# The down projection in two pairs of column blocks, with mixed pairs of contraction tiles, and three mixed pairs in ten gate/up units

## The chip, the core and the metric

One core of a Trainium2 chip runs the whole program, a two-layer decoder trunk in one launch. The metric is the device time of one execution in microseconds (us); the median of three runs is given. A profile is one execution recorded by the hardware profiler. Its engines are PE (TensorE: the matrix engine), DVE (VectorE), ACT (ScalarE), POOL (GpSimd) and SP, which issues most of the DMAs.

## What is computed

The input has 256 tokens of 2048 numbers, all float32. Each layer adds a normed mixer and a normed feed-forward part (FFN). Layer 0 has an SSD (Mamba-2) mixer, layer 1 has attention in a sliding window. Only the FFN is touched here:

```python
def swiglu(u, w_gate, w_up, w_down):
    return (jax.nn.silu(u @ w_gate) * (u @ w_up)) @ w_down
...
    ffn = swiglu(rmsnorm(h, g[2]), ffn_w_gate[layer], ffn_w_up[layer], ffn_w_down[layer])
    h = h + rmsnorm(ffn, g[3])
```

`w_gate` and `w_up` are 2048 x 5632, `w_down` is 5632 x 2048.

## The kernel before

**Products.** Tokens lie in two blocks of 128 (t = 0, 1). A weight tile of 128 contraction rows and 512 columns multiplies a block of tokens as three matmuls, since every float32 is held as a high and a low part in a shorter form: x_hi with w_hi, x_hi with w_lo, x_lo with w_hi. One such triple is called a product below.

**Weights.** `Weights` streams them. `specs` lists the loads in the order of use. `_load` fetches the next raw tile (512 KB: two contraction tiles of 512 columns) into one of RAWB = 5 buffers, up to four ahead; SP issues the DMAs in order. `_convert` makes `whi` with a cast on ACT and `wlo` with a subtraction on DVE, each in CVB = 4 buffers, three ahead of PE. A buffer is free for the next load or conversion when its last reader is done. A plain raw tile is one conversion of 128x1024, and 12 matmuls.

**The mixed form.** For two token blocks, two column blocks (in gate/up: 512 columns of gate and the same 512 of up) and a pair of contraction tiles (e, o), plain products would be eight. `mixed_unit` computes seven from sums of weights and differences of tokens (Strassen's scheme). Two raw tiles, `a` and `b`, carry the four weight tiles, each fetched by two DMAs of 256 KB. `_mixed` then gives four things to convert: `a` itself, t13 (one DVE add of 128x1024 from a and b), t24 (two DVE adds of 128x512, from t13, a and b), and `g`, half of b. They feed two, two, two and one products. The differences of tokens come once per layer from `mixed_x`, into `sx`. The seven banks p1 to p7 and `up1` are joined at the end of the unit by DVE (`L700` to `L703` once the mixed pairs are over, and `L708`), then SiLU on ACT and the product on DVE (`L712`).

**The FFN of a layer.** Gate and up go through 11 units of 512 columns. Unit 0 runs plain while h, the residual stream, is being updated (`a_first`); units 1 to 8 (S_FIRST to S_LAST) are mixed, with SPAIRS = 2 mixed pairs out of eight pairs of contraction tiles; units 9 and 10 are plain. The output of a unit is transposed on PE (`store_half`) and split into hh and hl; the part of units 8 and on goes to a second pair of tiles (`late`), which take the room of the mixed form's buffers. `mix_stage` then does down plain: four blocks of 512 columns, each with 44 contraction tiles and two token blocks. Behind each block, ACT takes the sum of squares (`squares`) and DVE multiplies with the norm's weights (`post`); the last block runs its last tiles token block by token block, so that the first one's norm factor is ready early. `add_residual` then updates h. `hook` starts small jobs (`mixed_x`, `store`) between weight tiles.

**Order.** A scheduler orders each engine's instructions at build time from the program order and priorities; at run time an engine runs its list in order, and semaphores hold it where data or a buffer is not ready. So an instruction that waits holds up everything behind it on its engine.

Of the kernel before, what the change touches and what calls it, by code (L numbers as in the profile page):

```python
# [30 lines left out]
SPAIRS = 2  # L31
S_FIRST, S_LAST = 1, 8
LATE = 8


class Weights:
# [40 lines left out]
    def _mixed(self, i, part):  # L77
# [57 lines left out]
def tile_yoco(ctx: ExitStack, tc: tile.TileContext, a: dict):  # L135
# [39 lines left out]

    def add_ffn(l):
        wg, wu = a["ffn_w_gate"][l], a["ffn_w_up"][l]
        for u in range(FF // CW):
            if not S_FIRST <= u <= S_LAST:
# [3 lines left out]
            for i in S_ORDER:  # L183
                e = SUB * i
                if i < SPAIRS:
                    for part, first, second in (("a", (wg, e), (wu, e + 1)), ("b", (wg, e + 1), (wu, e))):
                        specs.append(("s%d_%d" % (l, u), (part, *(wap(w, k, 1, CW * u, CW) for w, k in (first, second)))))
                else:
                    specs.append(("gate%d_%d" % (l, u), wap(wg, e, SUB, CW * u, CW)))
                    specs.append(("up%d_%d" % (l, u), wap(wu, e, SUB, CW * u, CW)))  # L190
        for c in range(4):
            add("down%d_%d" % (l, c), a["ffn_w_down"][l], KF, CW * c)
# [279 lines left out]
    h = hpool.tile([P, NT, D], F32, tag="h", name="h")  # L472
    for t in range(NT):
        nc.sync.dma_start(h[:, t, :], x[P * t : P * (t + 1), :])

    def mix_stage(key, xt, kts, layer, which, bk0=None, hook=None, lag=2):


        xh, xl = xt[:2]
        gpost = load_g(hpool, norm_w[layer, which], "gpost")  # L480
        ss = [hpool.tile([P, 4], F32, tag="mss%d" % t, name="mss", bufs=2) for t in range(NT)]
        bks = []

        def squares(bk, c, t):
            junk = hpool.tile([P, CW], mybir.dt.bfloat16, tag="junk", name="junk", bufs=2)
# [761 lines left out]
```

## Time and profile before

| | us |
|---|---|
| median of three runs | 2410.99 (2410.32 to 2412.8) |
| the profiled execution | 2411.38 |
| its span in the trace | 2409.7 |
| layer 0, SSD stage | 0 to about 690 |
| layer 0, gate and up | about 691 to 1187 |
| layer 0, down | about 1187 to 1416 |
| attention | 1417 to 1675 |
| layer 1, FFN | 1676 to 2401 |
| last norm, update of h, output | 2401 to 2409.7 |

The profile's page gives busy times, a picture of the span in slices, the DMA queues, the chain of waits and the costliest groups of instructions. The chain of waits starts at the last instruction and goes back, at each step, to what released it; the engine that holds most of it sets the time. A matmul's row in the trace is longer than the distance to the next one, because matmuls overlap in the engine's pipeline; the distance of the starts is the pace. Line numbers such as L672 are those of the code above. Buffer numbers are left out in the trace, so t13 and t24 both read `t`.

### The profile page before, as it was taken

To read this page: it belongs to the slowest core of one execution; us is meant where nothing else is said; L and a number is where in the kernel's file an instruction comes from. 1 tells how busy PE (TensorE), PEld (TensorE's weight loads), DVE (VectorE), ACT (ScalarE), POOL (GpSimd) and SP (SyncE) were. 2 spreads that over 40 slices of the span, in tenths; PEclk is the share of its full clock that TensorE was granted. 3 is DMA by queue.
4 is the path that set the end of the run, shared out by engine and by line. 5 is a ranking of instruction groups with operands and counts; after the bars stand their busy time and mean duration, and the time that the engine had idled before them with its cause. 6 is when DMAs were issued, how large, how long until landed. Compare 5 with 4: busy or idle time off the path is not lost.

```text
span 2409.7 us, 31424 instructions
## 1 busy us (share of the span) xinstructions
PE 2390.0 (99%) x11714; PEld 1980.7 (82%) x11714; DVE 1667.9 (69%) x2329; ACT 1279.7 (53%) x1805; POOL 87.2 (4%) x66
## 2 busy tenths in 40 slices
PE   9999999999999999999999999999999999999998
PEld 8888888888878888888888878777888888888887
DVE  6998878875577878875444468865878778554444
ACT  6566766654464545544444457755545555444443
POOL 2500100000000000000000000000000000000000
PEclk9999999999999999999999999999999999999999
DMA  7666666657656565666666664445665656666664
GB/s 223 184 202 192 186 190 191 183 178 244 193 165 200 177 216 168 216 201 185 207 193 194 194 191 153 128 126 163 191 202 177 214 177 199 201 189 207 194 194 143
DMA packets 285434, 453.80 MB, mean 188 GB/s; under 512 B 18000, under 2 KB 116560, under 8 KB 284512
## 3 DMA queue, kind: packets, MB, share of 16 engines
q1 hardware_dynamic: 284960, 451.39, 60.9%
q8 instruction: 92, 1.51, 0.3%
q14 instruction: 62, 0.51, 0.1%
q10 hardware_dynamic: 288, 0.33, 0.0%
q0 software_dynamic: 32, 0.07, 0.0%
HBM read 449.56 MB, written 2.16 MB: 187 GB/s over the span
## 4 chain that ended last, share of the span: by engine, by line
PE 97%; ACT 1%; DVE 1%; issue 0%; POOL 0%; DVEq 0%; POOLq 0%; ACTq 0%
PE bank L291 14%; PE bank L350 14%; PE bank L351 14%; PE bank L349 14%; PE bank L672 9%; PE bank L673 9%; PE bank L671 9%; PE bank L296 7%; PE bank L644 1%; PE bank L949 1%; PE bank L1125 1%; PE bank L1168 1%; DVE wlo L115 1%; PE bank L411 1%; ACT xx L270 0%; PE bank L1160 0%
## 5 line engine op out<-in xcount | busy, mean ns | idle before, releaser
L115 DVE TENSOR_TENSOR wlo<-raw,whi 128x1024 fp32r<-128x1024 f32 (+1 forms) x785 | 936.1, 1200 | 568.8 <-ACT whi L114 567.6
L114 ACT CAST whi<-raw 128x1024 fp32r<-128x1024 f32 (+1 forms) x785 | 811.1, 1036 | 828.9 <-PE bank L351 506.3
L291 PE MATMUL bank<-xx,whi 128*128 128x512 f32 (+1 forms) x1488 | 523.3, 396 | 0.0
L296 PE MATMUL bank<-xx,wlo 128*128 128x256 f32 (+1 forms) x1488 | 416.1, 285 | 0.0
L672 PE MATMUL bank<-wlo,xx 128*128 128x512 f32 x864 | 336.9, 390 | 0.3 <-DVE wlo L115 0.2
L671 PE MATMUL bank<-whi,xx 128*128 128x512 f32 x864 | 337.2, 393 | 0.0
L673 PE MATMUL bank<-whi,xx 128*128 128x512 f32 x864 | 336.9, 390 | 0.0
L291 PEld LDWEIGHTS bank<-xx,whi 128*128 128x128 f32 (+1 forms) x1488 | 276.6, 188 | 61.2 <-issue 0.4
L296 PEld LDWEIGHTS bank<-xx,wlo 128*128 128x128 f32 (+1 forms) x1488 | 280.2, 188 | 11.4 <-issue 7.0
L349 PE MATMUL bank<-whi,hh 128*128 128x512 f32 x512 | 199.3, 389 | 0.0
L351 PE MATMUL bank<-whi,hl 128*128 128x512 f32 x512 | 199.2, 389 | 0.0
L350 PE MATMUL bank<-wlo,hh 128*128 128x512 f32 x512 | 199.2, 389 | 0.0
L672 PEld LDWEIGHTS bank<-wlo,xx 128*128 128x128 f32 x864 | 162.3, 188 | 35.2 <-DVE wlo L115 2.1
L673 PEld LDWEIGHTS bank<-whi,xx 128*128 128x128 f32 x864 | 162.2, 188 | 34.2
L671 PEld LDWEIGHTS bank<-whi,xx 128*128 128x128 f32 x864 | 162.2, 188 | 32.8
L349 PE MATMUL bank<-whi,xx 128*128 128x512 f32 x416 | 162.6, 393 | 2.5 <-ACT xx L270 2.1
L351 PE MATMUL bank<-whi,xx 128*128 128x512 f32 x416 | 162.5, 392 | 0.9 <-DVE xx L271 0.9
L350 PE MATMUL bank<-wlo,xx 128*128 128x512 f32 x416 | 162.3, 391 | 0.5 <-DVE wlo L115 0.5
L114 ACT CAST whi<-t 128x1024 fp32r<-128x1024 f32 x64 | 67.2, 1050 | 107.7 <-DVE t L91 49.8
L351 PEld LDWEIGHTS bank<-whi,hl 128*128 128x128 f32 x512 | 96.1, 188 | 20.1
L350 PEld LDWEIGHTS bank<-wlo,hh 128*128 128x128 f32 x512 | 96.1, 188 | 20.0
L349 PEld LDWEIGHTS bank<-whi,hh 128*128 128x128 f32 x512 | 96.1, 188 | 19.7
(222 smaller groups left out, 3157.4 us busy)
## 6 DMA issues: line engine op xcount, KB each, us to landing
raw<-in_ffn_w_down_dram SPq DMA_DIRECT2D x176, 512.0 KB, 4.9
raw<-in_ssm_w_in_dram SPq DMA_DIRECT2D x161, 512.0 KB, 4.6
raw<-in_ffn_w_gate_dram SPq DMA_DIRECT2D x144, 512.0 KB, 4.5
raw<-in_ffn_w_up_dram SPq DMA_DIRECT2D x144, 512.0 KB, 4.6
raw<-in_ssm_w_out_dram SPq DMA_DIRECT2D x64, 512.0 KB, 4.8
raw<-in_ffn_w_gate_dram SPq DMA_DIRECT2D x64, 256.0 KB, 3.2
raw<-in_ffn_w_up_dram SPq DMA_DIRECT2D x64, 256.0 KB, 3.7
raw<-in_attn_w_q_dram SPq DMA_DIRECT2D x32, 512.0 KB, 3.4
```

Source lines behind the costliest of these rows:

```text
L114: self.pin(nc.scalar.copy(hi[:], src))
L115: self.pin(nc.vector.tensor_tensor(lo[:], src, hi[:].bitcast(F32), ALU.subtract))
L291: nc.tensor.matmul(o, wh, xx[:, kt, :, :].rearrange("p a t -> p (a t)"), start=(kt == 0), stop=(kt == kts - 1))
L296: nc.tensor.matmul(o[:, :T], wl, xx[:, kt, 0, :], start=False, stop=False)
L349: nc.tensor.matmul(o, sh, wh, start=(kt == 0), stop=False)
L350: nc.tensor.matmul(o, sh, wl, start=False, stop=False)
L351: nc.tensor.matmul(o, sl, wh, start=False, stop=(kt == kts - 1))
L411: nc.tensor.matmul(o[:], hi[:, kk, cs], xr[2][:, kt, :, :].rearrange("p a t -> p (a t)"), start=(kt == 0), stop=(kt == KD - 1))
L644: nc.tensor.transpose(pt[:, P * k : P * (k + 1)], scr[:, NT + t, P * k : P * (k + 1)], ident[:])
L671: nc.tensor.matmul(o, sh, wh, start=(n == 1), stop=False)
L672: nc.tensor.matmul(o, sh, wl, start=False, stop=False)
L673: nc.tensor.matmul(o, sl, wh, start=False, stop=(n == total[name]))
```

## The change

Three things change in the FFN of each layer.

Gate and up: units 1 to 10 are now mixed, with three mixed pairs (SPAIRS = 3) of eight. The order within a unit is a list: `UNIT` = A3 B3 M0 A4 B4 M1 A5 B5 M2 E A6 B6 A7 B7, where A and B are a plain raw tile of gate and of up, M a mixed pair, and E the first joining of the banks.

Down: the four column blocks go as two pairs, in the same form. `DOWN[0]` has six mixed pairs and 32 plain raw tiles: eight lead, then each M is followed by three. `DOWN[1]` has eight mixed pairs and 28 plain tiles: two lead, then each M is followed by two. Differences of tokens (now of hh and hl) are made by `mixed_x` for six and two pairs. The first half is kept in SBUF (`res`) after its norm weights, and copied back into banks near the end.

Room: hh and hl are now whole from the start, so h does not fit beside them. `spill_h` writes it to DRAM (`hd`) after `a_first` of unit 0 by two DMAs of 1 MB from POOL; `fetch_h` brings it back near the end of down, from POOL too. And t24 has no tile of its own any more: the two adds write into the raw tile `a`.

```diff
-SPAIRS = 2
-S_FIRST, S_LAST = 1, 8
-LATE = 8
+SPAIRS = 3
+def both(*pairs):
+    return [(c, i) for i in pairs for c in "AB"]
+def down_order(npairs, lead, each, last_a):
+    rest = range(npairs, KF // SUB)
+    a_ = [("A", i) for i in rest]
+    b_ = [("B", i) for i in rest]
+    n = lead + each * npairs
+    na = len(a_) - last_a
+    subs = a_[:na] + b_[: n - na]
+    seq = subs[:lead]
+    for i in range(npairs):
+        seq += [("M", i)] + subs[lead + each * i : lead + each * (i + 1)]
+    return seq + [("E", 0)] + a_[na:] + b_[n - na :]
+UNIT = both(3) + [("M", 0)] + both(4) + [("M", 1)] + both(5) + [("M", 2), ("E", 0)] + both(6, 7)
+DOWN = [down_order(6, 8, 3, 4), down_order(8, 2, 2, 4)]
...
-        t24 = self.spool.tile([P, 2, CW], F32, tag="t24", name="t24")
-        nc.vector.tensor_tensor(t24[:, 0, :], self.t13[:, 0, :], ta[:, 1, :], add)
-        nc.vector.tensor_tensor(t24[:, 1, :], t24[:, 0, :], tb[:, 0, :], add)
-        return t24[:]
+        nc.vector.tensor_tensor(ta[:, 1, :], self.t13[:, 0, :], ta[:, 1, :], add)
+        nc.vector.tensor_tensor(ta[:, 0, :], ta[:, 1, :], tb[:, 0, :], add)
+        return ta[:]
...
+    def spill_h():
+
+        for t in range(NT):
+            nc.gpsimd.dma_start(hd[:, t, :], h[1][:, t, :])
+        h[0].__exit__(None, None, None)
+
+    def fetch_h():
+        ht = open_h()
+        for t in range(NT):
+            nc.gpsimd.dma_start(ht[:, t, :], hd[:, t, :])
...
+        for p, made in ((0, range(6)), (1, range(6, 8))):
+            for i in made:
+                todo += [lambda i=i: make(i), None]
+            order = DOWN[p]
...
+                pp.item(item, terms)
+                if todo and item[0] in "AB":
+                    f = todo.pop(0)
+                    if f is not None:
+                        f()
+                if terms is not None and item[0] == "A" and order[n + 1][0] == "B":
+                    for t in range(NT):
+                        whole(0, t)
+                    if p == 0:
+                        keep(0)
+                    else:
...
+                        mix.done([pp.bk[name] for name in pp.OUT[:2]], 2)
+                        mix.sums()
+                        close()
+                        fetch_h()
...
+        def products(t):
+            for (kind, i), (hi, lo, _, _) in held:
+                pp.rest(kind, i, hi, lo, ts=(t,))
+            with tc.high_priority():
+                whole(1, t)
```

`pp.item` issues the matmuls of one entry of the list, `whole` adds the joined terms to a finished bank, and `make(i)` is `mixed_x` for down.

What the order of DVE looks like in a mixed unit, first before, from behind the t13 add of the first M to the last conversion of its t24 (`wlo<-t24`); the raw tile of `a` is raw_7197, that of `b` raw_7216, and raw_7291 and raw_7294 are a and b of the next M. `hl` is a half of the unit before, `scr` and `vh` (L708) its joining:

```order
L115 TENSOR_TENSOR wlo_7175<-raw_7154,whi_7174 128x1024 [waits DMAHW2_49,Activation_49]
L90 TENSOR_TENSOR t24_7264<-t13_7244,raw_7197 128x512 [waits DVE_49]
L91 TENSOR_TENSOR t24_7264<-t24_7264,raw_7216 128x512 [waits DMAHW6_49,DVE_49]
L115 TENSOR_TENSOR wlo_7201<-raw_7172,whi_7200 128x1024 [waits DMAHW3_49,Activation_49]
L238 TENSOR_TENSOR hl_6476<-bank_7190,hh_6475 128x4x128 [waits Activation_49]
L115 TENSOR_TENSOR wlo_7220<-raw_7197,whi_7219 128x1024 [waits Activation_49]
L115 TENSOR_TENSOR wlo_7247<-t13_7244,whi_7246 128x1024 [waits Activation_49]
L238 TENSOR_TENSOR hl_6476<-bank_7235,hh_6475 128x4x128 [waits Activation_49]
L708 TENSOR_TENSOR scr_6482<-bank_6990,scr_6482 128x512 [waits PE_49]
L708 TENSOR_TENSOR scr_6482<-bank_6982,scr_6482 128x512 [waits PE_49]
L87 TENSOR_TENSOR t13_7343<-raw_7291,raw_7294 128x1024 [waits DMAHW3_49,DMAHW5_49,DMAHW2_49,DVE_49]
L115 TENSOR_TENSOR wlo_7268<-t24_7264,whi_7267 128x1024 [waits Activation_49]
```

The two adds of t24 stand early, ahead of the joining, and they are the last to read raw_7197 but for the conversion of `a`; the t13 add of the next M stands ahead of the conversion of t24.

The same place after, in a unit, from the joining of the unit before (L842) to the last conversion of the first M's t24 (`wlo<-raw_7611`, after L112):

```order
L842 TENSOR_TENSOR scr_6481<-bank_7320,scr_6481 128x512 [waits PE_49]
L109 TENSOR_TENSOR t13_7666<-raw_7611,raw_7630 128x1024 [waits DMAHW7_49,DMAHW6_49,DMAHW1_49]
L136 TENSOR_TENSOR wlo_7634<-raw_7611,whi_7633 128x1024 [waits Activation_49]
L842 TENSOR_TENSOR vh_6775<-bank_7338,vh_6775 128x512 [waits DVE_49,PE_49]
L842 TENSOR_TENSOR vh_6775<-bank_7342,vh_6775 128x512 [waits PE_49]
L260 TENSOR_TENSOR hl_6480<-bank_7649,hh_6479 128x4x128 [waits Activation_49]
L846 SCALAR_TENSOR_TENSOR scr_6481<-vh_6775,rs_6752,scr_6481 128x512 [waits DVE_49]
L846 SCALAR_TENSOR_TENSOR scr_6481<-vh_6775,rs_6766,scr_6481 128x512 [waits DVE_49]
L136 TENSOR_TENSOR wlo_7669<-t13_7666,whi_7668 128x1024
L111 TENSOR_TENSOR raw_7611<-t13_7666,raw_7611 128x512
L112 TENSOR_TENSOR raw_7611<-raw_7611,raw_7630 128x512 [waits DMAHW0_49,DVE_49]
L136 TENSOR_TENSOR wlo_7691<-raw_7611,whi_7690 128x1024 [waits Activation_49]
```

The joining now stands ahead of t24, both adds write into raw_7611, and the conversion behind them is the last reader of that raw tile.

After, in the same unit, from the second M (a: raw_7708, b: raw_7711) to the third (a: raw_7795, b: raw_7798):

```order
L112 TENSOR_TENSOR raw_7708<-raw_7708,raw_7711 128x512 [waits DMAHW6_49,DVE_49]
L136 TENSOR_TENSOR wlo_7760<-t13_7757,whi_7759 128x1024 [waits Activation_49]
L136 TENSOR_TENSOR wlo_7780<-raw_7708,whi_7779 128x1024 [waits Activation_49]
L136 TENSOR_TENSOR wlo_7802<-raw_7711,whi_7801 128x512 [waits Activation_49]
L136 TENSOR_TENSOR wlo_7812<-raw_7755,whi_7811 128x1024 [waits DMAHW0_49,Activation_49]
L136 TENSOR_TENSOR wlo_7822<-raw_7775,whi_7821 128x1024 [waits DMAHW1_49,Activation_49]
L109 TENSOR_TENSOR t13_7840<-raw_7795,raw_7798 128x1024 [waits DMAHW5_49,DMAHW3_49,DMAHW2_49]
L136 TENSOR_TENSOR wlo_7832<-raw_7795,whi_7831 128x1024 [waits Activation_49]
L136 TENSOR_TENSOR wlo_7843<-t13_7840,whi_7842 128x1024 [waits Activation_49]
L111 TENSOR_TENSOR raw_7795<-t13_7840,raw_7795 128x512 [waits DVE_49]
L112 TENSOR_TENSOR raw_7795<-raw_7795,raw_7798 128x512 [waits DMAHW4_49,DVE_49]
L136 TENSOR_TENSOR wlo_7863<-raw_7795,whi_7862 128x1024 [waits Activation_49]
```

The t13 add of the third M (L109) comes behind the conversion of the second's t24 (`wlo_7780`), with three others between, and it reads raw_7798, the fifth raw tile after raw_7708.

DVE in unit 0 of layer 0, where `mixed_x` makes its first input, before (`sy`) and after (`yf`):

```order
L115 TENSOR_TENSOR wlo_6646<-raw_6585,whi_6645 128x1024 [waits DMAHW7_49,DVE_49,PE_49]
L223 TENSOR_REDUCE ms_6750<-ss_6741 128x1
L223 TENSOR_REDUCE ms_6764<-ss_6755 128x1
L633 TENSOR_TENSOR sy_6809<-xx_6471 128x512
L224 TENSOR_SCALAR ms_6750<-ms_6750 128x1 [waits DVE_49]
L224 TENSOR_SCALAR ms_6764<-ms_6764 128x1 [waits DVE_49]
```

```order
L136 TENSOR_TENSOR wlo_6645<-raw_6584,whi_6644 128x1024 [waits DMAHW7_49,DVE_49,PE_49]
L245 TENSOR_REDUCE ms_6749<-ss_6740 128x1
L245 TENSOR_REDUCE ms_6763<-ss_6754 128x1
L660 TENSOR_TENSOR yf_6816<-xx_6475 128x512 [waits DMASW2_49,DMASW1_49]
L246 TENSOR_SCALAR ms_6749<-ms_6749 128x1 [waits DVE_49]
L246 TENSOR_SCALAR ms_6763<-ms_6763 128x1 [waits DVE_49]
L136 TENSOR_TENSOR wlo_6651<-raw_6642,whi_6650 128x1024 [waits DMAHW0_49,Activation_49]
```

The add now waits for DMASW1 and DMASW2, the two spills; the conversion `wlo_6651` stands behind it.

POOL at the same place, after, with the two norm factors (L267) of the update of h ahead of the spills, and those of unit 0 behind:

```order
L267 TENSOR_TENSOR rs_6452<-ms_6450,neghalf_74 128x1 [waits DMAHW2_49,DMAHW3_49,DMAHW1_49,DMAHW4_49,DMAHW0_49,DMAHW5_49,DMASW0_49,DMAHW6_49,DVE_49,DMAHW7_49,PE_49,Pool_49]
L267 TENSOR_TENSOR rs_6471<-ms_6469,neghalf_74 128x1 [waits DVE_49]
L505 DMA hd_5555<-h_5559 128x2048 [waits DMAHW7_49,DVE_49]
L505 DMA hd_5555<-h_5559 128x2048 [waits DMAHW2_49,DVE_49]
L250 TENSOR_TENSOR rs_6752<-ms_6749,neghalf_74 128x1 [waits DVE_49]
L250 TENSOR_TENSOR rs_6766<-ms_6763,neghalf_74 128x1 [waits DVE_49]
```

Before, the rows at L505 are not there and the others follow one another.

## Rows read from the trace of the kernel before

**Rows 1.** The page: busy time by engine, and the chain of waits by engine.

```profile
PE 2390.0 (99%) x11714; PEld 1980.7 (82%) x11714; DVE 1667.9 (69%) x2329; ACT 1279.7 (53%) x1805; POOL 87.2 (4%) x66
...
PE 97%; ACT 1%; DVE 1%; issue 0%; POOL 0%; DVEq 0%; POOLq 0%; ACTq 0%
```

**Rows 2.** Timeline of PE in plain down: start, duration, engine, line, operation.

```profile
1249.71 0.39 PE L350 MATMUL bank<-wlo,hh 128*128 128x512 f32 x1
...
1261.95 0.39 PE L350 MATMUL bank<-wlo,hh 128*128 128x512 f32 x1
```

**Rows 3.** Windows: stretch, length, busy (count) of PE, PEld, DVE, ACT, POOL; PEclk.

```profile
714.00:1187.00 473.00, 472.80 (x2127) 391.06 (x2126) 344.40 (x377) 237.67 (x261) 1.70 (x2) 1.00 0.63 196
738.00:781.00 43.00, 42.80 (x193) 35.08 (x193) 31.47 (x34) 21.18 (x23) 0.00 (x0) 1.00 0.63 196
1200.00:1410.00 210.00, 210.00 (x929) 173.87 (x928) 99.12 (x88) 85.54 (x91) 0.00 (x0) 1.00 0.63 193
```

**Rows 4.** The page's groups: a mixed-form matmul line.

```profile
L672 PE MATMUL bank<-wlo,xx 128*128 128x512 f32 x864 | 336.9, 390 | 0.3 <-DVE wlo L115 0.2
```

**Rows 5.** The tiles t13 and t24: their instructions, and idle time before them.

```profile
L114 ACT CAST whi<-t x64: 1040/1051/1056, 736.7 to 2038.8; 128x1024 fp32r<-128x1024 f32 x64
...
L87 DVE TENSOR_TENSOR t<-raw x32: 1211/1224/1228, 730.3 to 2027.4; 128x1024 f32<-128x1024 f32 x32
...
L91 DVE TENSOR_TENSOR t<-t,raw x32: 686/692/694, 733.2 to 2038.0; 128x512 f32<-128x512 f32 x32
...
  DMA raw<-in_ffn_w_up_dram: 29.5, 18
```

**Rows 6.** Timeline of VectorE from 776 to 826 us.

```profile
783.88 1.22 DVE L87 TENSOR_TENSOR t<-raw 128x1024 f32<-128x1024 f32 x1
785.01 1.22 DVE L115 TENSOR_TENSOR wlo<-t,whi 128x1024 fp32r<-128x1024 f32 x1
786.15 1.28 DVE L708 TENSOR_TENSOR vh<-bank,vh 128x512 f32<-128x512 f32 x2
787.35 1.41 DVE L712 SCALAR_TENSOR_TENSOR scr<-vh,rs,scr 128x512 f32<-128x512 f32 x2
...
815.64 1.23 DVE L87 TENSOR_TENSOR t<-raw 128x1024 f32<-128x1024 f32 x1 [1.70 <-DMA raw<-in_ffn_w_up_dram]
```

**Rows 7.** Timeline of the DMA queue SP: weight loads of two b tiles.

```profile
779.43 0.33 SPq L70 DMA_DIRECT2D raw<-in_ffn_w_gate_dram  x1
...
811.25 0.33 SPq L70 DMA_DIRECT2D raw<-in_ffn_w_gate_dram  x1
```

**Rows 8.** The raw tiles from 776 to 800 us: landing times.

```profile
DMA to landing us min/median/max: 2.8/3.6/5.7
```

**Rows 9.** Timeline of VectorE at the first mixed input of layer 0.

```profile
704.39 0.74 DVE L533 SCALAR_TENSOR_TENSOR h<-bank,rs,h 128x512 f32<-128x512 f32 x1
...
713.73 0.68 DVE L633 TENSOR_TENSOR sy<-xx 128x512 f32<-128x512 f32 x1
...
714.63 1.22 DVE L115 TENSOR_TENSOR wlo<-raw,whi 128x1024 fp32r<-128x1024 f32 x1
```

**Rows 10.** Timeline of PE in the same stretch.

```profile
720.37 0.39 PE L350 MATMUL bank<-wlo,xx 128*128 128x512 f32 x1
```

**Rows 11.** DMA issues: count, size, median us to landing.

```profile
crow<-cumd SPq DMA_DIRECT2D x32, 256.0 KB, 3.7
gpost<-in_norm_w_dram SPq DMA_DIRECT2D x4, 1024.0 KB, 7.5
...
h<-in_x_dram SPq DMA_DIRECT2D x2, 1024.0 KB, 8.7
...
cumd<-scr POOLq DMA_DIRECT2D x1, 64.0 KB, 4.4
```

**Rows 12.** Chain of waits at the kernel's end: start, us, what.

```profile
2401.50 0.70 ACT junk L486 x2
```

**Rows 13.** Chain of waits between layer 0 and attention.

```profile
1420.18 0.52 POOL rs L245
```

More of the change, by code (lines that the diff above doesn't have):

```diff
@@ L178, in add_ffn @@
         for u in range(FF // CW):
-            if not S_FIRST <= u <= S_LAST:
+            if u == 0:
                 add("gate%d_%d" % (l, u), wg, KD, CW * u)
@@ L182, in add_ffn @@
                 continue
[L183 to L192, printed above, removed]
+            add_pairs("unit%d_%d" % (l, u), UNIT, (wg, CW * u), (wu, CW * u))
+        wd = a["ffn_w_down"][l]
+        for p in range(2):
+            add_pairs("down%d_%d" % (l, p), DOWN[p], (wd, 2 * CW * p), (wd, 2 * CW * p + CW))
     add_ffn(0)
@@ L476, in mix_stage @@
     def mix_stage(key, xt, kts, layer, which, bk0=None, hook=None, lag=2):
         xh, xl = xt[:2]
[L480 to L485, printed above, removed]
-            nc.scalar.activation(junk[:], bk[t][:], AF.Square, accum_out=ss[t][:, c : c + 1])
-        def post(bk, c, t):
-            return nc.vector.tensor_tensor(bk[t][:], bk[t][:], gpost[:, CW * c : CW * (c + 1)], ALU.mult)
@@ L528, in mix_stage @@
-        return bks, rs
+        mix = Mix(layer, which)
+        for c in range(3):
+            if c == 0 and bk0 is not None:
+                bk = bk0
+            else:
+                bk = a_form("%s%d" % (key, c), xt, kts, hook=hook if c == 0 else None)
+            mix.done(bk, c)
+        mix.sums()
+        bk = [bank() for _ in range(NT)]
+        nsub = kts // SUB
+        held = []
+        for s in range(nsub):
+            hi, lo, _, per = W.next("%s%d" % (key, 3))
+            if s < nsub - lag:
+                for kk in range(per):
+                    a_mm(bk, xh, xl, hi, lo, kk, SUB * s + kk, kts, 0, CW)
+            else:
+                held.append((hi, lo, s, per))
@@ L530, in add_residual @@
+        def products(t):
+            for hi, lo, s, per in held:
+                for kk in range(per):
+                    a_mm(bk, xh, xl, hi, lo, kk, SUB * s + kk, kts, 0, CW, ts=(t,))
+        mix.last(bk, products)
+        return mix
     def add_residual(mix, t, c):
-        bks, rs = mix
-        hs = h[:, t, CW * c : CW * (c + 1)]
-        nc.vector.scalar_tensor_tensor(hs, bks[c][t][:], rs[t][:, 0:1], hs, ALU.mult, ALU.add)
+        hs = h[1][:, t, CW * c : CW * (c + 1)]
+        nc.vector.scalar_tensor_tensor(hs, mix.banks[c][t][:], mix.rs[t][:, 0:1], hs, ALU.mult, ALU.add)
@@ L549, in step @@
                 update(c, t)
[L550 removed]
+                to_xt(h[1][:, t, CW * c : CW * (c + 1)], t, c, g, xt)
                 update(c + 1, t)
@@ L575, in row_factor @@
     def row_factor():
-        return [norm_stats(hpool, h, t) for t in range(NT)]
+        return [norm_stats(hpool, h[1], t) for t in range(NT)]
     def to_row(rs):
```

326 lines of the change are left out of this document (187 added, 139 removed).

## The prediction

> **What bounds the kernel now.** First the page [rows 1]: TensorE (PE) is busy 99% of the span and the chain of waits, followed back from the last instruction, is 97% PE. Busy time alone would not prove a bound, since a matmul's row lasts 0.39 us while the next starts 0.23 us after it. So I took the starts [rows 2]: 55 plain down matmuls from 1249.71 to 1261.95, that is 54 steps of 0.2267 us without a hole. The same pace holds in each FFN stage [rows 3]: PE is busy 472.80 of 473.00 us in gate/up of layer 0 and 210.00 of 210.00 in down, at a granted clock of 1.00. VectorE has 344.40 of 473.00 us there, but only 99.12 of 210.00 in down, ScalarE and the DMA queues less. Last, what PE waits for in the mixed form that exists already: 0.2 us in all, for 864 matmuls of each of the three kinds [rows 4]. So a matmul that goes away is worth its 0.2267 us, until a conversion comes too late.
>
> **What is removed.** A mixed pair has seven products where the plain form has eight, and a product is three matmuls. Gate/up had 8 units x 2 pairs = 16 mixed pairs per layer and gets 10 x 3 = 30; down had none and gets 6 + 8 = 14. That is 28 products less per layer, 56 in two, 168 matmuls: 168 x 0.2267 = **-38.1 us**, all on the path. Transposes and the SSD and attention stages keep their counts.
>
> **What is added on engines with room.** Per added mixed pair VectorE gets a t13 add (1.22 us) and two t24 adds (0.69 each) [rows 5], and its fourth conversion is of half size, which I put at 0.69 like an add of that size. A unit of before took VectorE 31.47 of 43.00 us [rows 3]; a unit of after has one pair more and two plain tiles less: 1.22 + 1.38 + (3 x 1.22 + 0.69) - 2 x 1.22 = + 4.5, so 36.0 us. PE's unit goes to 43.0 - 3 x 0.2267 = 42.3 us. VectorE is at 85%: not a bound, but every wait on it is nearer. In down, M and two plain tiles cost VectorE 2.6 + 4.3 + 2.4 = 9.3 us against 45 matmuls = 10.2 us of PE. As VectorE's order holds the work of several units at once, I cost these at nothing while their lead lasts; the next two parts say where it may not.
>
> **The slot loop.** This is the main unknown. t24 is now written into the raw tile of `a`, so that tile stays taken until the last conversion of t24 (lo24). There are five raw tiles; with M and two plain tiles the order of loads is a, b, A, B, a', b', and b' takes the tile of a. So lo24 of one M releases the two 256 KB loads of the next b', and the next t13 add waits for these. Before, the tile was free with the second t24 add. What the trace gives for such a pair: the one issued from 811.25 let its t13 add start at 815.64, after 1.70 us of idle, so 4.4 us; the one issued from 779.43 was there when its add began at 783.88, so at most 4.4 [rows 6, 7]. A single landing was 2.8 at least and 3.6 in the middle [rows 8], and the second load goes out 0.4 later, which makes 3.2 to 4.0. I take 3.2 to 4.4. Behind the landing VectorE's new order has two patterns, both in the listing: t13, t24, t24, lo13, lo24, which is 1.22 + 0.69 + 0.69 + 1.14 + 1.14 = 4.9 us (1.14 from start to start of a conversion and what follows it [rows 6]), and t13, lo a, lo13, t24, t24, a cast (1.05 [rows 5]), lo24, some 7.1. The loop is then 8.1 to 9.3 us or 10.3 to 11.5, against 10.2 us of PE from M to M (45 matmuls).
>
> In a unit the first loop is of the short kind (gain 0.9 to 2.1 us) and the second of the long kind (loss 0.1 to 1.3); after the third M four plain tiles refill the lead. The lead at a unit's start: VectorE has the two adds on vh, the split of a hidden half, two products, lo13, two t24 adds, a cast and lo24, 1.28 + 0.69 + 1.41 + 1.14 + 1.38 + 1.05 + 1.14 = 8.1 us [rows 5, 6], less some 0.08 for each of six that follow one another; it can start 0.3 us before the unit does (the first bank ends three matmuls early, and a row lasts 0.39), so it ends some 7.4 to 7.8 us into the unit. PE needs lo24 after 36 matmuls, 8.16 us: lead 0.4 at least. So a unit ends between + 2.5 and + 0.1 us: nothing by these rows, and I take 0.1 us of stall for uneven landings, 2 us for 20 units (ends 0 and 6). Down's second half has seven loops per layer that alternate, 10.4 us in the mean at the slow end: 0.5 us per layer (0 to 2). Its first half has M and three plain tiles, 12.9 us, with a' and b' both behind lo24 (0.8 us more), so 11.1 to 12.3 us, and the making of mixed inputs (some 2.5 us each) inside the first two: 0.5 us per layer (0 to 3). Sum **+4**, ends 0 and 16. A loop that bites also empties the DMA queue ahead of b', which pulls it to the short landings.
>
> **The spill of h.** h now goes to DRAM by two POOL transfers of 1 MB, and VectorE's first mixed-input add waits for both. That add stood at 713.73 and the conversion behind it at 714.63; the last update of h began at 704.39 and ended 705.1 [rows 9], and the tile of that conversion, found by its place in PE's order, was taken at 720.37 [rows 10]. No 1 MB transfer of POOL is in the trace. Bounds: 7.5 to 8.7 us for 1 MB from SP; and the one POOL transfer, 64 KB, took 4.4 us where 256 KB from SP took 3.7, so 0.7 us more or somewhat above [rows 11]. Landing at 712.6 to 715; the conversion would end by 717.2, 3 us before its use. In layer 1 the order is the same. I take 0.3 us per layer, **+0.6** (ends 0 and 8, if two transfers at once take twice the time).
>
> The rule that speaks against this is in the Trainium skill, page "SBUF — State Buffer", section "SBUF: two separate sides": a DMA issued from GpSimd needs descriptors that GpSimd writes through a port pair that some VectorE operations lock, so it can starve while VectorE is busy. The one POOL transfer here, 4.4 us for 64 KB, neither proves nor excludes it; by that rule the spill lands some conversions later, which is the second rival below.
>
> **The fetch of h.** Issued about 16 us of PE (six plain tiles) before the down stage ends, needed after its last product. Two transfers at 7.5 to 8.7, each with the extra of POOL, end before that. 0 (0 to 4).
>
> **The ends of the stages.** Down's last chain gets one more add per token block before its squares. At the kernel's end it lies bare, since squares follow the last product there [rows 12]: + 0.7, the price of an add of that size. Between layer 0 and attention the factor of the second block came only at 1420.18, behind mask work on POOL [rows 13], which may cover it: + 0.5 (0 to 1.5). At the border of down's two halves the banks are read by VectorE and ScalarE while others are free: + 0.5 (0 to 2).
>
> **Sum.** Made against the profiled span, 2409.7 us, and 2411.4 with what lies around it; the median of three is 2410.99, 0.4 lower. 2411.0 - 38.1 + 4 + 0.6 + 0.7 + 0.5 + 0.5 = 2379.2. With all lower ends 2373.6, with all upper ends 2405. **I say 2379**, own range 2373 to 2386.
>
> **Rivals.**
> *The slot loop bites in every unit.* For it: 18 of 32 t13 adds of before already waited for their load, 29.5 us in all [rows 5]. Against it: PE waited 0.2 us for that. With 1 us per unit and 1 us per loop in down (24 loops), 20 + 24 = 44 instead of 4 would end at 2419; with half of it, which is the likelier size, 2397. Chance 0.17 for 2386 to 2406.
> *Spill or fetch late.* If the spill lands only at 720 to 725, VectorE stands in front of its add and PE runs out of conversions after 4.5 us of lead: 3 to 6 us per layer, and the fetch as much at each end. 2411 - 38 + 6 + 2 x 8 = 2395. The trace shows nothing of that size for a POOL transfer. Chance 0.08, inside the same stretch.
> *No gain, by slow landings.* Each us that the pair of loads takes beyond 4.4 lengthens two loops in each of 20 units, 14 loops in down's second halves and 10 in the first: 64 us per us. At 4.4 about 4 us are lost; of the gain 32 us are then left, and gone when the mean pair takes 4.4 + 32 / 64 = 4.9 us. The slowest single landing of [rows 8] was 5.7; if the mean pair took 5.3, the result would be 2379 + 0.9 x 64 = 2437. Against it: both pairs that can be read took no more than 4.4. Chance 0.06 for slower, 0.04 for the rim within 0.2%.
> *VectorE as bound.* At 36.0 of 42.3 us it is not one on average; only together with waits, and then it is the first rival.
>
> **Chances.** About 0.2% (4.8 us) is what a measurement of this kernel can tell from no change. Forecast 0.65, the first two rivals 0.25, none 0.04, slower 0.06: faster 0.90, same 0.04, slower 0.06. The range takes the forecast, and most of the first two rivals: 2372 to 2397.
>
> **What would show it.** PE's busy time down by 38 us, idle before the products of t24 and 13 below 5 us in all. If the loop bites, the changed page shows PE waiting for wlo in the mixed lines, about equal in each unit and always at the second and third M, with t13 waiting for its load just before. If the spill is late, one gap of some us near 720 and near 1715, with the first mixed-input add ended by a POOL transfer. If the fetch is late, a gap after the last down product. The prediction is wrong if PE's idle time grows by over 10 us.

## The result, and the profile after

The changed kernel takes 2421.4 us (six runs, 2417.6 to 2422.7) against 2411.2: 1.0038 times as long, 95% interval 1.0025 to 1.0051. I had said 2379 and given slower a chance of 0.06. The profiled execution took 2418.9 us, its span is 2417.2.

The page of after answers to [rows 1] and [rows 4]: busy time by engine, the chain of waits, then two groups, a mixed-form matmul line in down and the t13 add (instructions, busy, mean ns, idle time before and what ended it).

```profile
PE 2371.9 (98%) x11546; PEld 1952.8 (81%) x11546; DVE 1972.0 (82%) x2781; ACT 1378.1 (57%) x1951; POOL 91.9 (4%) x74
...
PE 81%; DVE 8%; DMA 4%; ACT 3%; issue 2%; SPq 0%; ACTq 0%; DVEq 0%; POOL 0%; POOLq 0%
...
L692 PE MATMUL bank<-wlo,hh 128*128 128x512 f32 x564 | 223.5, 396 | 13.2 <-DVE wlo L136 13.1
...
L109 DVE TENSOR_TENSOR t<-raw 128x1024 f32<-128x1024 f32 x88 | 107.5, 1221 | 49.0 <-DMA raw<-in_ffn_w_down_dram 41.1
```

The 168 matmuls are gone (11714 to 11546) and PE is busy 18 us less, yet the chain is 81% PE where it was 97%. The rest is mostly VectorE (8%, before 1%), loads from DRAM (4%), which the chain did not name before, and ScalarE (3%). The t13 adds waited 41.1 us for loads of the down weights; before, down had no t13 adds.

Where it lies is read from the starts of the matmuls in the timelines: a stage goes from its first start to the last one, with one step of 0.2267 us added behind the last matmul. For down of layer 0, first and last matmul, before and then after:

```profile
1176.52 0.39 PE L349 MATMUL bank<-whi,hh 128*128 128x512 f32 x1
...
1417.12 0.47 PE L351 MATMUL bank<-whi,late 128*128 128x512 f32 x1
```

```profile
1168.74 0.48 PE L691 MATMUL bank<-whi,hh 128*128 128x512 f32 x1
...
1419.37 0.39 PE L693 MATMUL bank<-whi,hl 128*128 128x512 f32 x1
```

All stages (us):

| stretch | before | after | before, less the matmuls removed |
|---|---|---|---|
| gate and up, layer 0 | 485.5 | 476.9 | 476.0 |
| gate and up, layer 1 | 486.0 | 478.1 | 476.5 |
| down, layer 0 | 240.8 | 250.9 | 231.3 |
| down, layer 1 | 240.3 | 250.7 | 230.7 |
| attention, between the two | 257.7 | 259.7 | |
| behind the last matmul | 8.4 | 9.2 | |

So gate and up brought 16.5 of 19.0 us, and each down stage, which should have brought 9.5 (42 matmuls), lost 10. Windows show it too (length, then busy us and count of PE, PEld, VectorE, ACT, POOL, then the clock and the DMA share): a stretch of gate/up and one in down's second half, after; then the latter before.

```profile
745.00:1160.00 415.00, 414.24 (x1859) 341.19 (x1858) 375.25 (x415) 233.31 (x263) 0.00 (x0) 1.00 0.58 196
1284.00:1384.00 100.00, 92.70 (x383) 73.16 (x381) 75.36 (x79) 46.73 (x55) 0.00 (x0) 0.97 0.51 163
```

```profile
1284.00:1384.00 100.00, 100.00 (x443) 82.81 (x442) 48.30 (x45) 41.22 (x45) 0.00 (x0) 1.00 0.63 193
```

PE stands 7.3 us in 100, VectorE 24.6 (busy 75.36), and the DMA engines do less than before (0.51 against 0.63). None of them is full: something goes in a circle.

PE did 60 matmuls fewer in this stretch (383 against 443), which is 13.6 us, so 7.3 us of standing are not all. Part of the rest is the clock: two times, each behind waits of PE of about 1 us, the granted clock was 0.50 for 3.4 us, the lower of its two levels (1.2 GHz), from 1314.0 and from 1361.8. The same window view of the first, after:

```profile
1314.00:1317.40 3.40, 3.40 (x10) 2.62 (x9) 2.95 (x3) 1.10 (x2) 0.00 (x0) 0.50 0.74 167
```

Matmuls start 0.43 us apart there, in place of 0.23. Each layer's down has two such stretches, before has none. At both times the chain of waits runs through loads, so by it the lower clock follows from the stall and does not set the pace.

The chain names the circle (start, us, what; one turn in down's second half, and the load that opens the next):

```profile
1297.77 1.24 DVE wlo L136
...
1299.02 0.33 SPq L92
...
1299.40 6.09 DMA raw<-in_ffn_w_down_dram
...
1305.52 1.24 DVE t L109
...
1306.85 1.05 ACT whi L135
...
1309.07 0.70 DVE raw L111
...
1309.79 0.70 DVE raw L112
...
1310.60 1.05 ACT whi L135
...
1311.67 1.24 DVE wlo L136
...
1313.30 5.18 DMA raw<-in_ffn_w_down_dram
```

From the conversion of t24 that ends at 1299.01 to the issue of the next b, 6.09 us to its landing, t13, a cast, two t24 adds, a cast, and the conversion of t24 again, which ends at 1312.91: 13.9 us for an M and two plain tiles that PE does in 10.2. PE is not in this turn at all. It is the slot loop of the prediction.

### The profile page after: what moved, and what is told of

Same layout as the page of the kernel before. It is cut to its first block, busy times and chain, and to the rows that moved or that the text cites. A ratio compares the mean times of both kernels' runs of the same rounds, so it can differ in the third digit from the quotient of the medians.

```text
span 2417.2 us, 31988 instructions
## 1 busy us (share of the span) xinstructions
PE 2371.9 (98%) x11546; PEld 1952.8 (81%) x11546; DVE 1972.0 (82%) x2781; ACT 1378.1 (57%) x1951; POOL 91.9 (4%) x74
## 4 chain that ended last, share of the span: by engine, by line
PE 81%; DVE 8%; DMA 4%; ACT 3%; issue 2%; SPq 0%; ACTq 0%; DVEq 0%; POOL 0%; POOLq 0%
PE bank L313 14%; PE bank L692 13%; PE bank L693 13%; PE bank L691 13%; PE bank L318 7%; PE bank L372 5%; PE bank L373 5%; PE bank L371 5%; DMA raw<-in_ffn_w_down_dram 4%; DVE wlo L136 4%; ACT whi L135 2%; DVE t L109 1%; DVE raw L112 1%; DVE raw L111 1%; PE bank L1079 1%
## 5 line engine op out<-in xcount | busy, mean ns | idle before, releaser
L135 ACT CAST whi<-raw 128x1024 fp32r<-128x1024 f32 (+1 forms) x873 | 865.4, 1009 | 665.8 <-DVE raw L112 201.5
L136 DVE TENSOR_TENSOR wlo<-raw,whi 128x1024 fp32r<-128x1024 f32 (+1 forms) x873 | 1002.7, 1168 | 290.8 <-ACT whi L135 282.4
L691 PE MATMUL bank<-whi,xx 128*128 128x512 f32 x980 | 385.0, 393 | 0.0
L692 PE MATMUL bank<-wlo,xx 128*128 128x512 f32 x980 | 382.5, 390 | 2.0 <-DVE wlo L136 2.0
L693 PE MATMUL bank<-whi,xx 128*128 128x512 f32 x980 | 382.2, 390 | 0.0
L692 PE MATMUL bank<-wlo,hh 128*128 128x512 f32 x564 | 223.5, 396 | 13.2 <-DVE wlo L136 13.1
L693 PEld LDWEIGHTS bank<-whi,xx 128*128 128x128 f32 x980 | 184.0, 188 | 37.9
L691 PEld LDWEIGHTS bank<-whi,xx 128*128 128x128 f32 x980 | 184.1, 188 | 37.5 <-ACT whi L135 0.2
L135 ACT CAST whi<-t 128x1024 fp32r<-128x1024 f32 x88 | 92.8, 1054 | 173.1 <-DVE t L109 149.5
L109 DVE TENSOR_TENSOR t<-raw 128x1024 f32<-128x1024 f32 x88 | 107.5, 1221 | 49.0 <-DMA raw<-in_ffn_w_down_dram 41.1
L136 DVE TENSOR_TENSOR wlo<-t,whi 128x1024 fp32r<-128x1024 f32 x88 | 107.4, 1221 | 2.0 <-ACT whi L135 0.3
L371 PE MATMUL bank<-whi,yh 128*128 128x512 f32 x256 | 100.1, 391 | 0.0
```

Source lines behind the costliest of these rows:

```text
L109: nc.vector.tensor_tensor(self.t13[:], ta[:], tb[:, 1:2, :].broadcast_to([P, 2, CW]), add)
L135: self.pin(nc.scalar.copy(hi[:], src))
L136: self.pin(nc.vector.tensor_tensor(lo[:], src, hi[:].bitcast(F32), ALU.subtract))
L371: nc.tensor.matmul(o, sh, wh, start=(kt == 0), stop=False)
L691: nc.tensor.matmul(o, s[0], wh, start=(n == 1), stop=False)
L692: nc.tensor.matmul(o, s[0], wl, start=False, stop=False)
```

## The experiments

All times are medians of three rounds, beside the kernel before on the same chip (2410.9 to 2411.7). The stage lengths are read as in the table above.

**Gate and up alone.** Down plain as before; h is fetched at the start of down.

```diff
-        for p in range(2):
-            add_pairs("down%d_%d" % (l, p), DOWN[p], (wd, 2 * CW * p), (wd, 2 * CW * p + CW))
+        for c in range(4):
+            add("down%d_%d" % (l, c), wd, KF, CW * c)
...
-            spool = tc.tile_pool(name="down%d" % layer, bufs=1, side="right")
-            W.spool = dp = spool.__enter__()
+            fetch_h()
...
-            mix = down_stage(layer, hid, todo, dp, lambda: spool.__exit__(None, None, None),
-                             2 if layer == 0 else CVB)
-            return mix
+            return mix_stage("down%d_" % layer, hid, KF, layer, 3, hook=hook, lag=2 if layer == 0 else CVB)
```

> Only the gate/up part of the change with the spill of h, which is fetched at the start of down; down is plain as before. Theory: gate/up brings 16.5 us (476.9 and 478.1 instead of 485.5 and 486.0 in the profile) and the loss lies in down alone, so 2395 +- 3. Rival (the spill or the fetch costs some of it, or gate/up hides a loss that falls to down): 2400 to 2411.

Measured: 2394.1 (ratio 0.9927, 0.9912 to 0.9941). Gate and up take 477.5 and 477.4 us, down 241.3 and 240.4 as before. So the loss is down's alone, and spill and fetch cost nothing that this run can show.

**t24 in the tile of t13.**

```diff
-        nc.vector.tensor_tensor(ta[:, 1, :], self.t13[:, 0, :], ta[:, 1, :], add)
-        nc.vector.tensor_tensor(ta[:, 0, :], ta[:, 1, :], tb[:, 0, :], add)
-        return ta[:]
+        t = self.t13
+        nc.vector.tensor_tensor(t[:, 1, :], t[:, 0, :], ta[:, 1, :], add)
+        nc.vector.tensor_tensor(t[:, 0, :], t[:, 1, :], tb[:, 0, :], add)
+        return t[:]
```

> The changed kernel, but the two adds of t24 write into the tile of t13 (which is converted by then), so the raw tile of a is free after the first t24 add and not after the conversion of t24. Nothing else differs. Theory (slot loop: conversion of t24 -> loads of the next b -> t13 -> conversion of t24): the loop of down loses the cast and the conversion, about 2.5 us of 12.3, and comes to about the 10.2 us of PE; each down stage falls from 250.7 to 232 to 238 us, the whole to 2382 to 2394. Rival (VectorE is the bound of down, 9.3 of 10.2 us, and the waits only show it): no more than 5 us saved, 2415 to 2421. Second rival (the DMA queue can't deliver the down weights faster in this order): 2410 to 2421.

Measured: 2473.6 (1.0254, 1.0239 to 1.0269), worse than all that was expected. Down did gain (245.0 and 245.2 us), but gate and up went to 510.1 and 510.7. VectorE's timeline in a unit of this run shows why (start, us, operation, idle before):

```profile
844.38 1.22 DVE L109 TENSOR_TENSOR t<-raw 128x1024 f32<-128x1024 f32 x1
846.79 1.23 DVE L137 TENSOR_TENSOR wlo<-t,whi 128x1024 fp32r<-128x1024 f32 x1 [1.20 <-ACT whi L136]
848.05 0.69 DVE L112 TENSOR_TENSOR t<-t,raw 128x512 f32<-128x512 f32 x1
848.77 0.69 DVE L113 TENSOR_TENSOR t<-t,raw 128x512 f32<-128x512 f32 x1
850.66 1.23 DVE L137 TENSOR_TENSOR wlo<-t,whi 128x1024 fp32r<-128x1024 f32 x1 [1.19 <-ACT whi L136]
851.80 4.09 DVE L137 TENSOR_TENSOR wlo<-raw,whi 128x512 fp32r<-128x512 f32 x4
855.81 1.22 DVE L109 TENSOR_TENSOR t<-raw 128x1024 f32<-128x1024 f32 x1
```

One tile now carries t13 and t24, so its add, cast, conversion, two adds, cast and conversion follow one another, with VectorE idle through both casts (1.20 and 1.19 us), and four more conversions stand before the next t13: 11.4 us from t13 to t13, against 10.2 of PE. No load is waited for in it; this run made another loop in place of the one it removed, and says little on the first.

**Mixed pairs of down from other weights.** Three runs change only from where the two raw tiles of a mixed pair in down are loaded: gate and up; q; gate alone.

```diff
-        (wa, ca), (wb, cb) = blocks
+        (wa, ca), (wb, cb) = m or blocks
...
+                      m=((wg, 2 * CW * p), (wu, 2 * CW * p)))       # first run
...
+                      m=((wq, 2 * CW * p), (wq, 2 * CW * p + CW)))  # second run
...
+                      m=((wg, 2 * CW * p), (wg, 2 * CW * p + CW)))  # third run
```

> The changed kernel, but in down the two raw tiles of each mixed pair are read from the gate and up weights instead of the down weights, the same bytes in the same number of transfers, so the output is another one. The plain tiles of down are read as before. It asks why the pair of loads lands after 5.3 to 6.5 us in down where it takes 3.4 in gate/up. Theory (the place of the down weights in DRAM, rows of 8 KB of which 2 KB are read): landing falls to about 3.4 us, the loop to about 9.8 us, down to 232 us, the whole to 2382. Rival (the load of the queue in down, whatever the source: the plain tiles behind share the engines): landing stays over 5 us and the whole at 2417 to 2422.

> As the run that reads the mixed pairs of down from gate and up, but from the attention's q weights, whose rows are as long as those of the down weights (8 KB, of which 2 KB are read); the output is another one. It asks whether the distance of the rows makes the landing slow, or the down tensor itself. Theory (distance of the rows): the pair of loads lands after 5.3 to 6.5 us again, the whole is at 2412 to 2422. Rival (the tensor itself, where it lies or that the plain tiles read it too): about 3.4 us and 2379 to 2385.

> The mixed pairs of down read from the gate weights alone: one tensor and neighbouring column blocks, as with the down and the q weights, but rows 22 KB apart instead of 8 KB; the output is another one. The earlier run with gate and up differed from the one with q in two things, the distance of the rows and two tensors instead of one. Theory (distance of the rows): 2377 to 2384, as with gate and up. Rival (two loads of a pair from one tensor, in neighbouring blocks, get in each other's way): 2410 to 2422, as with q.

Measured: 2379.4 (0.9864, 0.9849 to 0.9879), 2419.4 (1.0034, 1.0021 to 1.0046) and 2378.3 (0.9862, 0.9845 to 0.9878). The first is the number that I had forecast for the change. Windows of the same stretch of down, in this order:

```profile
1284.00:1384.00 100.00, 100.00 (x441) 82.47 (x440) 84.92 (x88) 57.78 (x67) 0.39 (x1) 1.00 0.61 202
```

```profile
1284.00:1384.00 100.00, 90.63 (x376) 70.63 (x374) 75.01 (x79) 46.74 (x56) 0.00 (x0) 0.98 0.50 159
```

```profile
1284.00:1384.00 100.00, 100.00 (x443) 82.68 (x442) 85.74 (x89) 56.66 (x64) 0.00 (x0) 1.00 0.62 205
```

PE is full with the gate's weights (100.00 of 100 us) and stands 9.4 us with q's. VectorE's work for a mixed pair is the same in all three, and where the loads come sooner it does more of it (84.92 and 85.74 us busy against 75.01), so it was not the bound. The t13 add and the loads that it waits for, in the run with gate and up (the DMA queue, then VectorE), and for the changed kernel the same two views:

```profile
1290.99 0.33 SPq L92 DMA_DIRECT2D raw<-in_ffn_w_gate_dram  x1
```

```profile
1294.49 1.23 DVE L109 TENSOR_TENSOR t<-raw 128x1024 f32<-128x1024 f32 x1
```

```profile
1299.02 0.81 SPq L92 DMA_DIRECT2D raw<-in_ffn_w_down_dram  x2
```

```profile
1305.52 1.23 DVE L109 TENSOR_TENSOR t<-raw 128x1024 f32<-128x1024 f32 x1 [3.65 <-DMA raw<-in_ffn_w_down_dram]
```

A pair of 256 KB loads is there 3.5 us after its first issue in one case and 6.5 us in the other. Bytes, transfers and queue are the same. Gate rows are 5632 numbers (22 KB) long, those of down and q 2048 (8 KB); each load of a pair takes 2 KB of each of 128 rows. One tensor or two made no difference, and two tensors of each row length behave alike, so of what was varied the distance of the rows is left.

It is not the distance alone. In the attention stage of the changed kernel, loads of 512 KB from q (pieces of 1 KB) and from the output projection (pieces of 2 KB), both with rows of 8 KB, landed sooner than the 6.1 us of the 512 KB loads of down. Issues on the page (KB each, median us to landing):

```profile
raw<-in_attn_w_q_dram SPq DMA_DIRECT2D x32, 512.0 KB, 3.5
raw<-in_attn_w_o_dram SPq DMA_DIRECT2D x32, 512.0 KB, 4.3
```

There they mostly went out some us apart, one or two under way at a time; in down four loads go out within 2 us, the pair first. So the slow landing is shown for short pieces from such rows with several loads under way. Why they come slower then, and whether 8 KB counts as a distance or as a power of two, the runs don't show. The Trainium skill, page "DMA: Bandwidth & Descriptors", section "Latency and other measured facts", reports slower copies at row distances of 2 MB and more, powers of two, and takes memory channels that many rows share for the likely reason, unverified. 8 KB is far below its table, and no run here shows whether the reason is the same.

**Four plain tiles between the mixed pairs.**

```diff
-DOWN = [down_order(6, 8, 3, 4), down_order(8, 2, 2, 4)]
+DOWN = [down_order(5, 8, 4, 4), down_order(5, 2, 4, 4)]
...
-        for p, made in ((0, range(6)), (1, range(6, 8))):
+        for p, made in ((0, range(5)), (1, range(0))):
```

> The changed kernel, but down has five mixed pairs in each half, with four plain tiles between two of them instead of three and two. Then the loads of the next a and b take tiles that are free before the conversion of t24, so the loop is gone, at the price of four products more per layer, 24 matmuls in all, 5.4 us. Theory: down at about 236 us a layer, the whole at 2384 to 2392. Rival (VectorE or the rate of the DMA queue): VectorE has the same work per M and more time, the queue the same bytes; if the queue's rate is the limit, down stays above 245 and the whole above 2408.

Measured: 2399.6 (0.9948, 0.9932 to 0.9965); down 242.3 and 243.5 us. Between the two answers, and my premise was wrong. The chain:

```profile
1299.50 7.20 DMA raw<-in_ffn_w_down_dram
...
1315.10 8.59 DMA raw<-in_ffn_w_down_dram
...
1332.09 9.22 DMA raw<-in_ffn_w_down_dram
```

With four between, a' and b' take the tiles of b and of the first plain tile, which come free still later than a. The loads of a', b' and plain tiles then go out together, and the one that the t13 add waits for lands after up to 9.2 us.

**Rows of 4 KB.** In down, a holds one contraction tile for both column blocks, b the next; the sums are formed from the halves. A tile is then one load of 512 KB in place of two of 256 KB, so two things change at once, the length of the pieces and the number of loads. The second run reads the plain tiles between the mixed pairs in the same way, where one load stays one load (its edit is not shown).

```diff
+                if wa is wb:
+                    specs.append((key + "M", ("a", wap(wa, e, 1, ca, 2 * CW))))
+                    specs.append((key + "M", ("b", wap(wa, o, 1, ca, 2 * CW))))
+                    continue
...
+                nc.vector.tensor_tensor(self.t13[:, 0, :], ta[:, 0, :], ta[:, 1, :], add)
+                nc.vector.tensor_tensor(self.t13[:, 1, :], tb[:, 1, :], ta[:, 1, :], add)
...
+            nc.vector.tensor_tensor(ta[:, 1, :], self.t13[:, 0, :], tb[:, 1, :], add)
+            nc.vector.tensor_tensor(ta[:, 0, :], ta[:, 1, :], tb[:, 0, :], add)
```

> The changed kernel, but in down the raw tile a holds one contraction tile for both column blocks (rows of 4 KB, one transfer of 512 KB instead of two of 256 KB), and b the next contraction tile; the casts and subtractions of the first conversion and the t13 add go in two halves each, about 0.3 us more for VectorE and 0.2 us more for ScalarE per mixed pair. Theory (short pieces of rows 8 KB apart make the landing slow): landing at 3.6 to 4.6 us, the loop at about 10.5, down at 232 to 238 us a layer, the whole at 2380 to 2392. Rival (this tensor is slow to read at any length of row): landing over 5 us, the whole over 2408.

> As the run with rows of 4 KB for the mixed pairs of down, and the plain tiles between them are read so too: one contraction tile for both column blocks (128 rows of 4 KB) in place of two contraction tiles for one block; the last ten plain tiles of each half (three or five of each block) stay as they were. The same bytes, products and conversions. Theory (short pieces of rows 8 KB apart make the loads late, the ring of five raw tiles can't cover it): with the neighbours faster too, the mean landing in down falls from 5.3 to 4.5 us or less, down from 239 to 231 to 236 us a layer, the whole to 2380 to 2390. Rival (the half-size operations of the first conversion and of t13 cost what is still lost in that run, or the ring is too short at any landing): 2393 to 2400.

Measured: 2395.9 (0.9934, 0.9919 to 0.9949) with the mixed pairs alone, 2391.9 (0.9923, 0.9908 to 0.9938) with the plain tiles between them too; down 239.2 and 238.3, then 240.2 and 239.1 us. Over half of the loss is gone. What share the longer pieces have and what share the single load, the runs don't separate. Reading the neighbours in 4 KB too gives nothing clear of noise: the two intervals overlap, and the stage lengths are of the fastest execution of the first run and the slowest of the second. In the chain of the second run the loads took 3.9 to 5.9 us, but the loop grew on VectorE's side, where the first conversion and t13 go in halves: 5.9 and 8.0 us from the landing to the end of t24's conversion, where the changed kernel has 5.1 and 7.4.

**t24 in its own tile, in down.**

```diff
+        t24 = ta
+        if self.own24:
+            t24 = self.spool.tile([P, 2, CW], F32, tag="t24", name="t24")
...
```

> The changed kernel, but in down t24 has a tile of its own again, so the raw tile of a is free at the second t24 add; gate/up is as in the changed kernel. Loads and their sources are unchanged, the landing stays at 5.3 to 6.5 us. Theory (the loop: conversion of t24 -> loads -> t13 -> conversion): a cast and a conversion, 2.3 us, leave the loop, which comes from 12.3 to about 10 us against PE's 10.2; down at 232 to 240 us, the whole at 2382 to 2398. Rival (the rate of the loads alone sets the pace): 2412 to 2421.

> As the run before, and t24 has its own tile in down, so a is free two conversions' time earlier. Theory (the residence of the raw tiles sets the pace, landing is one part of it and the hold by t24 another): no worse than the run before, 2377 to 2388, with down at 231 to 234 us. Rival (own tile brings only a new order, as in the run with t24 alone in its own tile, 4 us): the same as the run before within 4 us.

Measured: 2417.0 (1.0020, 1.0011 to 1.0030), down 250.7 and 250.4; with the rows of 4 KB in mixed pairs and plain tiles besides 2397.8 (0.9947, 0.9931 to 0.9964), where the rows alone gave 2391.9. Four us less in one case, six more in the other, and each time the intervals overlap: to hold a for less time at its end does not help. The chain of the first shows the loads still in the loop, now behind other conversions:

```profile
1304.80 5.78 DMA raw<-in_ffn_w_down_dram
1310.70 1.23 DVE t L109
...
1317.55 5.14 DMA raw<-in_ffn_w_down_dram
1322.81 1.23 DVE t L109
```

So my loop was one of several through the same five tiles. An estimate: with four tiles to load per 10.2 us, each can be kept 5 x 10.2 / 4 = 12.75 us on average, and a load of 5 to 6 us leaves some 7 for waiting and converting.

**Two more raw tiles in down.**

```diff
-                t = self.pool.tile([P, 2, CW], F32, tag="raw", name="raw", bufs=RAWB)
+                if key.startswith("down") and ap[0] == "a":
+                    t = self.spool.tile([P, 2, CW], F32, tag="rawa", name="raw", bufs=2)
+                else:
+                    t = self.pool.tile([P, 2, CW], F32, tag="raw", name="raw", bufs=RAWB)
...
```

> The changed kernel, with the raw tile a of each mixed pair of down in two buffers of its own, so that seven raw tiles are in use there instead of five; the loads, their sources and their number are unchanged. To make room, the making of mixed inputs and the joined terms of down use the buffer of t13. Theory (five raw tiles can't cover landings of 5 to 6 us, each M holding two of them from issue to the conversion of t24): with two more, b' no longer waits for the conversion of t24, down comes to 231 to 237 us a layer, the whole to 2378 to 2392. Rival (the loads from rows 8 KB apart can't be faster in the mean, whatever the number of tiles): 2408 to 2421.

> As the run before, and the mixed pairs of down are read in rows of 4 KB (as in the earlier run with that alone, 2396). Theory: both take a part of the same wait, so this is 2378 to 2388 and not slower than the run before. Rival (the halved operations of the first conversion and of t13 lengthen the chain): 3 to 8 us slower than the run before.

Measured: 2386.4 (0.9898, 0.9881 to 0.9914), down 235.2 and 235.2 us; with rows of 4 KB besides 2377.2 (0.9858, 0.9843 to 0.9873), down 231.0 and 231.5, which is the count of matmuls. Windows of down, two more tiles alone, then both:

```profile
1284.00:1384.00 100.00, 96.38 (x424) 79.07 (x423) 84.57 (x97) 56.12 (x65) 0.00 (x0) 1.00 0.60 185
```

```profile
1284.00:1384.00 100.00, 100.00 (x443) 82.72 (x442) 88.15 (x113) 59.79 (x77) 1.01 (x2) 1.00 0.59 194
```

PE goes from 92.70 to 96.38 to 100.00 us of 100, with loads from the same weights. Both levers act on one thing, the time that a raw tile is taken against the number of them, and together they beat both kernels by 34 and 44 us.

## Why the prediction was wrong, step by step

**What bounds, and what is removed.** Right. Where nothing waits, a matmul was worth 0.2267 us: the best run has all 168 of them as gain, within 0.8 us in each stage.

**VectorE and ScalarE.** Right that they are no bound, with the unit's sum too low: I had 85% in a unit and 91% in down, and VectorE was busy 375.25 of 415.00 us in gate and up, 90%. PE was full beside it in three runs, with VectorE at 85 to 88% in down.

**The slot loop: mechanism right, one term mis-sized.** The step that failed is "I take 3.2 to 4.4" for the landing of a pair. Both measured pairs [rows 6, 7] and the landings [rows 8] were loads of gate and up, and I used them for down. For units they held. Here the DMA queue and VectorE in a unit of after:

```profile
836.01 0.33 SPq L92 DMA_DIRECT2D raw<-in_ffn_w_gate_dram  x1
...
845.03 0.33 SPq L92 DMA_DIRECT2D raw<-in_ffn_w_gate_dram  x1
```

```profile
839.92 1.21 DVE L109 TENSOR_TENSOR t<-raw 128x1024 f32<-128x1024 f32 x1
...
842.50 1.22 DVE L136 TENSOR_TENSOR wlo<-t,whi 128x1024 fp32r<-128x1024 f32 x1
...
848.56 1.22 DVE L109 TENSOR_TENSOR t<-raw 128x1024 f32<-128x1024 f32 x1
```

3.9 and 3.5 us from the first issue to the t13 add; loops of 9.0 and 11.0 us, inside the 8.1 to 9.3 and 10.3 to 11.5 of the prediction, and 0.9 and 1.6 us lost per layer against 1 forecast.

In the second half of down the pair took 5.3 to 6.5 us; the chain behind it is close to what I had (5.1 and 7.4 us, I had 4.9 and 7.1); so loops of 10.5 to 10.9 and 13.3 to 13.9, 12.3 in the mean of layer 0 and 12.4 of layer 1, some 2.1 over PE's 10.2. Seven of them lost 14.6 and 15.7 us, and the first half, with pairs up to 7.5, lost the other 4 to 5: 19.6 and 20.0 us per layer where I had put 1. That is the 40 us. My own sign of being wrong came with it: PE's idle time grew from 19.7 us (2409.7 - 2390.0) to 45.3 (2417.2 - 2371.9), by more than 10.

The first rival was half right: the loop bit in every turn in down, some 1.7 us for each of 24, and hardly in the units. The "no gain" rival had the mechanism and the turning point (4.9 us for the mean pair), but its price of 64 us per us counted the units too. With the 24 loops of down alone, a mean pair of 5.9 us costs 24 x 1.5 = 36 us over my sum, an estimate near the 42 that were missing. It got 0.06 because "both pairs that can be read took no more than 4.4", and neither of them was a load of down. A hint stood on the page of before: 512 KB of down weights landed after 4.9 us, of gate weights after 4.5, a small thing while loads went out one by one. That a stalled loop "empties the DMA queue ahead of b', which pulls it to the short landings" was half right: the queue was empty, and the pair still took 5.3 to 6.5 us.

**The spill.** Right, at nothing. The same VectorE rows as [rows 9], after: the last update of h, and the first mixed input.

```profile
705.23 0.74 DVE L592 SCALAR_TENSOR_TENSOR h<-bank,rs,h 128x512 f32<-128x512 f32 x1
...
714.59 0.68 DVE L660 TENSOR_TENSOR yf<-xx 128x512 f32<-128x512 f32 x1
```

```profile
hd<-h POOLq DMA_DIRECT2D x4, 1024.0 KB, 4.5
...
h<-hd POOLq DMA_DIRECT2D x4, 1024.0 KB, 7.2
```

The add does not wait. 1 MB from POOL to DRAM landed after 4.5 us, far below my bounds of 7.5 to 8.7 (which were loads by SP, among its weight loads). The Trainium skill, page "DMA: Bandwidth & Descriptors", section "Anatomy of one DMA — SWDGE (gpsimd) path", gives 2.0 us and the bytes at 436 GB/s, which for 1 MB makes an estimate of 4.4 us: the trace agrees for the spill, not for the fetch (7.2). The rule of the Trainium skill, page "SBUF — State Buffer", section "SBUF: two separate sides", on descriptors that starve behind some VectorE operations did not show in these spills, with VectorE at work on float32 additions and conversions all through. The second rival falls. The fetch was hidden, as forecast.

**The ends.** At the kernel's end 0.8 us (0.7 forecast): the new add stands before the squares in the chain of after.

```profile
2408.21 0.71 DVE bank L742
...
2409.00 0.70 ACT junk L529 x2
```

Between layer 0 and attention 2.0 us instead of 0.5 (1.5 at most). About 1.5 of it is the clock. Right behind the stage border, where PE had waited for the update of h and the norm, the granted clock was 0.50 (the lower level) for 3.4 us, and before it was 1.00 there. The window, after:

```profile
1423.20:1426.60 3.40, 3.40 (x11) 2.73 (x11) 2.02 (x4) 0.78 (x2) 0.00 (x0) 0.50 0.00 0
```

Four runs with this form of down have no such stretch at this place (four plain tiles between, q, rows of 4 KB in the mixed pairs, rows and own tile): they took 258.1 to 258.7 us from layer 0 to layer 1's gate and up, 0.4 to 1.0 over before. So the add itself cost what I had put.

## What to carry to other kernels

A duration belongs to its source: before a transfer's time is used in a sum, take it from the rows that read the same tensor with the same row length, and if the trace has none in the new pattern, let the range run to the worst of the neighbours. When a change makes loads wait for the end of the work on an earlier tile, the number of buffers, the landing and the work form a loop, and the loop is compared with the time of the engine that it feeds. Here the loop was opened by more buffers and by faster loads; to move the release within it only found the next loop.

## What was not expected of the hardware

Two loads of 256 KB, each in 128 pieces of 2 KB, with more loads right behind, land later when the pieces lie 8 KB apart than at 22 KB: 5.3 to 6.5 us against 3.4 to 4.8 for the pair of them, from an idle queue, on two tensors of each kind. In the attention stage, with fewer loads under way, 512 KB in pieces of 2 KB from rows of 8 KB took 4.3 us in the middle. In pieces of 4 KB from the 8 KB rows of down the single 512 KB loads on the chain took 3.9 to 5.9 us. A 1 MB store from POOL to DRAM took 4.5 us while the weight stream ran; SP's loads of 1 MB took 7.6 and 8.6 in the same execution. Behind some waits of PE of about 1 us the granted clock was 0.50 for 3.4 us, two times in each layer's down.
